# Down projections of two gated MLPs: where the folds of the weight blocks stand in VectorE's queue

## The chip, the cores and the metric

One core of one Trainium2 chip runs the whole kernel. The metric is the device time of one execution in microseconds; 2590.62 us is the median of three runs of the kernel before (2589.14 to 2591.91). An execution under the profiler took 2588.23 us, of which the profile shows a span of 2586.4 us from the first to the last instruction.

## The reference, cut to what matters

A trunk of two layers (a gated linear attention and a Fourier mixer), each followed by a gated MLP with a width-3 convolution, on 1024 latent and 128 context tokens of width 1024. The change lies in the last product of the MLP, which is computed once per layer:

```python
def conv_ffn(h, w_up, conv_w, conv_b, w_down, rows):
    a, g = jnp.split(h @ w_up, 2, axis=-1)
    ...
    return (jax.nn.silu(a) * g) @ w_down
```

`w_down` is 2816 x 1024 (2816 = 22 blocks of 128), and its product is added to the residual stream with a gate per channel.

## The kernel before

`ffn(l, ...)` computes the MLP of layer l. Its second half, the down projection, multiplies by a Strassen-Winograd scheme: the 1152 tokens are cut in two halves, the 22 row blocks of `w_down` in even and odd ones (11 pairs, `NP`), its 1024 columns in two halves. That gives four kinds of weight block (kind 0 to 3; `wd[kind, j]` is a 128 x 512 block of pair j), and seven products in place of eight. The loop over `steps` runs the first five products in the order `a2`, `s1`, `s4`, `a1`, `s2`, each over both slices of 288 tokens of its half, and then `s3` and `g2` once for each slice. Each step walks the 11 pairs, j = 0 to 10; a pair of a step is called a block here.

A block of a step needs three things before TensorE (PE) can run its 24 matmuls (4 column groups m, 2 slices s, 3 matmuls each on lines 97 to 99, since every fp32 operand is a high and a low part):

- a **stationary operand** (`stationary`): ScalarE (ACT) copies the weight block to its high part (L1073, `wd`), VectorE (DVE) subtracts to get the low part (L1074, `wd`, called "lo" here). Six buffers (tag "wh") hold them, so they run up to six blocks ahead of PE.
- a **moving operand** for each slice (`moving`): SyncE (SP) loads the slice (L1082, `hr`), ACT makes the high part (L1083, `hh`), DVE the low part (L1084, `hl`). Two pairs of buffers hold them, so `hh` and `hl` of block j + 2 have to wait until PE is through with block j.
- in `s1` and `s4`, and at the end of `s2`, a **fold** of the weight blocks in place (`fold`, L1064 on DVE): `s1` needs kind 2 plus kind 3 (one fold a pair); `s4` needs kind 1 minus (the sum less kind 0), two folds a pair, the second reading the first. A fold is one 128 x 512 instruction, or two of 128 x 256 for pair 10, whose halves lie in two pages: 12 fold instructions in `s1`, 24 in `s4`, in each layer.

At the end of each step, its sums are added into the residual pages: DVE reads PSUM or ACT's copy of it (L1165, `xd`; the copies are L1162, `room`). The next step's matmuls into the same PSUM bank wait for that.

The order of the work on an engine is set when the program is built: a scheduler takes instructions by priority as they become ready in its own model, and `tc.high_priority()` puts the operands of all blocks ahead of the matmuls. `tc.issue_after(ins)` keeps the instructions of its block behind `ins` in their engine's queue, and no more. Each engine then runs its queue strictly in that order. Before, all folds of a step are kept behind one instruction, `made[kind]`, the last lo of the step before (`behind`, fetched at j = 0):

```python
if j == 0 and what in ("s1", "s4"):
    behind = made[{"s1": 1, "s4": 2}[what]].ins
if what == "s1":
    with tc.issue_after(behind):
        fold(2, 3, ALU.add, j)
```

Weight blocks of kinds 1 to 3 are loaded in `a2`, those of kind 0, which `s4`'s first fold reads, during `s1` (`loads`, L1025 and L1034 on SP).

Of the kernel before, what the change touches and what calls it, by code (L numbers as in the profile page):

```python
# [15 lines left out]
F32 = mybir.dt.float32  # L16
# [4 lines left out]
ALU = mybir.AluOpType  # L21
# [24 lines left out]
def trunk(tc, a, o):  # L46
    nc = tc.nc
    V, S, G, PE = nc.vector, nc.scalar, nc.gpsimd, nc.tensor
# [16 lines left out]
    def mm_ps(name):  # L65
        return pp.tile([P, 512], F32, tag="mm", bufs=3, name=name)

    def at_ps(name):
        return pp.tile([P, 512], F32, tag="at", bufs=4, name=name)
# [156 lines left out]
    def feed(x, first, key, acc=None):  # L226

        n = key[1] - key[0]
        if first:
            accs[key] = sb.tile([P, CH], F32, tag="kt", bufs=3, name=f"acc{key[0]}") if acc is None else acc  # L230
            S.activation(accs[key][:, :n], x, AF.Square)
        else:
            sq = t15("sq")[:, :n] if n > SUB else sb.tile([P, SUB], F32, tag="sb", bufs=4, name="sq")[:, :n]
            S.activation(sq, x, AF.Square)
            V.tensor_tensor(accs[key][:, :n], accs[key][:, :n], sq, op=ALU.add)  # L235
# [743 lines left out]
    def ffn(l, xp, rs, xd, after, ahead=None, w=None, stages=None):  # L979
# [57 lines left out]
        def key(th, s):  # L1037
            return th * HT + s * SUB, th * HT + (s + 1) * SUB
# [22 lines left out]
        def fold(x, y, op, j, reverse=False):  # L1061

            for (c, xx), (_, yy) in zip(wd[x, j], wd[y, j]):
                V.tensor_tensor(xx, *((yy, xx) if reverse else (xx, yy)), op=op)  # L1064

        made = {}

        def stationary(kind, j, wt=None):
            if wt is None:
                wt = sb.tile([P, 1032], F32R, tag="wh", bufs=6, name=f"wd{l}")[:, :1024]  # L1070
            for c, x in wd[kind, j]:
                hi, lo = wt[:, c], wt[:, 512:][:, c]
                S.activation(hi, x, AF.Copy)  # L1073
                made[kind] = V.tensor_tensor(lo, x, hi.bitcast(F32), op=ALU.subtract)  # L1074
            return wt

        def moving(name, ss, j):
            hi, lo = (t30(n, F32R).rearrange("p a b -> p (a b)")[:, :HT] for n in ("hh", "hl"))
            for s in ss:
                c = slice(s * SUB, (s + 1) * SUB)  # L1080
                raw = t15("hr")[:, :SUB]
                nc.sync.dma_start(raw, hd[j][names.index(name), s])  # L1082
                S.activation(hi[:, c], raw, AF.Copy)  # L1083
                V.tensor_tensor(lo[:, c], raw, hi[:, c].bitcast(F32), op=ALU.subtract)  # L1084
            return hi, lo
# [12 lines left out]
        def room_for_kept():  # L1098
            pgs = [page(f"keep{i}", F32R) for i in range(7)]
            slots = [pg[:, 1024 * i:1024 * i + 1024] for pg in pgs for i in range(2)]  # L1100
            slots.insert(10, sb.tile([P, T], F32R, tag="w4", bufs=1, name="keep")[:, :1024])
            kept.update(zip([("s3", j) for j in range(NP)] + [("g2", j) for j in range(4)], slots))

        def products(m, what, ss, wt, hi, lo, first, last):
            for s in ss:
                c = slice(s * SUB, (s + 1) * SUB)
                mm3(pss[m, s][:, :SUB], (wt[:, m * P:(m + 1) * P], wt[:, 512 + m * P:512 + (m + 1) * P]),
                    (hi[:, c], lo[:, c]), first, last, skip=True)
        for n, (what, name, kind, (mh, th), ss) in enumerate(steps):
            if what in fresh:  # L1110
                for s in range(2):
                    for m in range(4):
                        pss[m, s] = at_ps("pd") if s else mm_ps("pd") if m < 3 else \
                            pp.tile([P, 512], F32, tag="md", bufs=1, name="pd")
            if ahead:
                ahead(n)
            elif n == 5:
                room_for_kept()
            held = []
            for j in range(NP):  # L1120
                for load, *args in loads.get((n, j), ()):
                    load(*args)
                with tc.high_priority():

                    if j == 0 and what in ("s1", "s4"):
                        behind = made[{"s1": 1, "s4": 2}[what]].ins

                    if what == "s1":
                        with tc.issue_after(behind):
                            fold(2, 3, ALU.add, j)  # L1130
                    elif what == "s4":
                        with tc.issue_after(behind):
                            fold(2, 0, ALU.subtract, j)
                            fold(1, 2, ALU.subtract, j)
                    wt = kept.get((what, j))
                    if wt is None or n < 7:
                        wt = stationary(kind, j, wt)
                    hi, lo = moving(name, ss, j)
                    if what == "s2":
                        fold(2, 3, ALU.subtract, j, reverse=True)  # L1140
                held.append((what, ss, wt, hi, lo, what in fresh and j == 0, j == NP - 1))

                if n < len(steps) - 1 or j != NP - 2:
                    for m in range(4):
                        for args in held:
                            products(m, *args)
                    held = []
                if n == 7 and j == 5:
                    norms = after(X, xp, rs, key(1, 0), key(0, 0))
                if n == 8 and j == 5:  # L1150
                    norms = after(X, xp, rs, key(1, 1))
                if n > 6 and j > 4 and j != 6 or n == 8 and j < 5:
                    next(norms, None)
            room = sb.tile([P, T], F32, tag="w4", bufs=1, name="room") if len(ss) > 1 else None
            for m in range(4):
                x = Xw(4 * mh + m)
                for s in ss:
                    t0, t1 = key(th, s)
                    got = pss[m, s][:, :SUB]
                    if s and room is not None:  # L1160
                        copied = room[:, m * SUB:(m + 1) * SUB]
                        S.activation(copied, got, AF.Copy)  # L1162
                        got = copied
                    for c0, c1, c in [(t0, t1, 0)] if t1 <= LAT else [(t0, LAT, 0), (LAT, t1, 1)]:
                        V.scalar_tensor_tensor(x[:, c0:c1], got[:, c0 - t0:c1 - t0], gate(4 * mh + m, c),  # L1165
                                               x[:, c0:c1], op0=ALU.mult, op1=ALU.add)
            if final_of[mh, th] == what:
                for s in ss:
                    k = key(th, s)
                    for m in range(4 * mh, 4 * mh + 4):  # L1170
                        feed(Xw(m)[:, slice(*k)], k not in accs, k, acc1[s] if th else None)
# [8 lines left out]
    def after0(X, xp, rs, *keys):  # L1180
        for key in keys:
            save_x(xp, xs_dram, slice(*key))
        yield from rstd_steps(rs, *keys)
    xp, X, Xw, rs = ffn(0, xp, rs, xs, after0, fold_operands, early["w"], early["ops"])


# [77 lines left out]
    for pr_ in range(2):  # L1264
# [5 lines left out]
        for typ in range(2):  # L1270
# [15 lines left out]
            for i in range(6):  # L1286
                off = (i % 2) * 1024 + typ * 512
                hi, lo = (dat[i // 2][:, off + h:off + h + 256].rearrange("p (g n) -> p g n", g=2) for h in (0, 256))
# [11 lines left out]
        def pqv(pq, g, typ, hl, half):  # L1300
            i = (g * 2 + typ) * 4 + hl * 2 + half
            return pq[i // 6][:, (i % 6) * CH:(i % 6 + 1) * CH]
# [4 lines left out]
        for half in range(2):  # L1307
            tw = weight(a["dft_t"][half], 1024, f"dt{half}{pr_}")
            for typ in range(2):
# [5 lines left out]
                for g, ny in todo:  # L1315
# [12 lines left out]
                    else:  # L1328
                        hi, lo = pqv(pq, g, typ, 0, half), pqv(pq, g, typ, 1, half)
# [14 lines left out]
    for m in range(KT):  # L1344
        with tc.high_priority():
            raw = raw_w(a["fwo"][m], 1024, f"fo{m}")
            whl = [sb.tile([P, 1032], F32R, tag="wh", bufs=6, name=f"fw{i}") for i in range(2)]
            for typ in range(2):
# [5 lines left out]
                hi, lo = (w[:, typ * 512:typ * 512 + 512] for w in whl)  # L1354
# [17 lines left out]
        x = Xw(m)  # L1372
# [48 lines left out]
    for _ in norm:  # L1421
        pass
    ffn(1, xp, rs, xs, final)
    ctx.close()

# [133 lines left out]
```

## Time and profile before

| | before |
|---|---|
| median of 3 runs | 2590.62 us |
| the profiled execution | 2588.23 us |
| its span | 2586.4 us |
| PE busy | 2429.6 us, 94% |
| DVE busy | 1844.4 us, 71% |
| ACT busy | 1090.3 us, 42% |
| mean granted TensorE clock | 0.977 |
| the DVE folds, L1064 | 96 instructions, 88 + 8 |

Reading it: PE is the engine that is nearly always busy, so time is what keeps PE idle or slows its clock. A matmul of 288 columns follows the one before it after some 0.13 us at the full clock (granted 1.00, which is 2.4 GHz) and 0.24 us at the lower level (0.50, 1.2 GHz). The down projection of layer 0 runs from about 1260 to 1490 us, that of layer 1 from about 2297 us to the end. In the rows further down, a number in brackets is the idle time of the engine just before the instruction, with what ended it.

### The profile page before, as it was taken

What the parts mean: (1) busy time and instruction counts of PE and PEld (TensorE: products, weight loads), DVE (VectorE), ACT (ScalarE), POOL (GpSimd) and SP (SyncE); (2) the same over time, 40 slices, a digit from 0 to 9 for tenths busy, and PEclk for the clock granted to TensorE, in tenths of its full rate; (3) what the DMA queues carried; (4) which work ended last, traced back from release to release, by engine and by line L of the source; (5) the groups of instructions that cost most, each with busy time, mean ns of one, the idle gap of its engine ahead of it and who ended that gap; (6) DMA issues with size and microseconds to landing.
All of it is one profiled execution on the core that took longest, in us unless ns stands there. A gap on an engine that the chain in (4) does not pass through costs nothing. (4 is left out here: it accounts for less than half of the span.)

```text
span 2586.4 us, 46546 instructions
## 1 busy us (share of the span) xinstructions
PE 2429.6 (94%) x18122; PEld 2332.2 (90%) x18122; DVE 1844.4 (71%) x3339; ACT 1090.3 (42%) x2086; POOL 732.9 (28%) x548
## 2 busy tenths in 40 slices
PE   6999999988999999999989998999899999998997
PEld 5998988887999899999989996998899999998997
DVE  7647384666698677777766877287987777787676
ACT  5435343444364233333335564344533333333453
POOL 3435344543103334344100005330144444410000
PEclk9999999998999999999999998999999999999999
DMA  7213222104334443323754347343223232375334
GB/s 261 74 48 93 81 88 79 54 21 145 109 108 126 155 137 99 114 82 101 242 178 134 113 153 214 102 166 134 94 79 115 82 114 82 98 240 176 93 84 126
DMA packets 200972, 309.85 MB, mean 120 GB/s; under 512 B 18288, under 2 KB 142064, under 8 KB 200752
## 3 DMA queue, kind: packets, MB, share of 16 engines
q1 hardware_dynamic: 196528, 302.66, 36.8%
q10 hardware_dynamic: 4224, 4.23, 0.5%
q8 instruction: 142, 2.33, 0.4%
q14 instruction: 78, 0.64, 0.1%
HBM read 233.71 MB, written 73.11 MB: 119 GB/s over the span
## 5 line engine op out<-in xcount | busy, mean ns | idle before, releaser
L98 PE MATMUL pd<-hl,wd 128*128 128x288 f32 x1112 | 331.9, 301 | 28.7 <-DVE hl L1084 28.5
L99 PE MATMUL pd<-hh,wd 128*128 128x288 f32 x1112 | 329.9, 300 | 0.0
L97 PE MATMUL pd<-hh,wd 128*128 128x288 f32 x1112 | 317.6, 299 | 5.5 <-ACT hh L1083 3.2
L98 PEld LDWEIGHTS pd<-hl,wd 128*128 128x128 f32 x1112 | 213.7, 192 | 31.2 <-DVE hl L1084 30.7
L809 POOL TENSOR_TENSOR s<-wa,s 128x512 fp32r<-128x512 f32 x114 | 157.3, 1380 | 278.4 <-ACT s L808 278.4
L1084 DVE TENSOR_TENSOR hl<-hr,hh 128x288 fp32r<-128x288 f32 x308 | 138.3, 454 | 133.8 <-ACT hh L1083 133.5
L1083 ACT ACTIVATE hh<-hr 128x288 fp32r<-128x288 f32 x308 | 133.4, 437 | 233.7 <-PE pd L98 218.8
L97 PEld LDWEIGHTS pd<-hh,wd 128*128 128x128 f32 x1112 | 205.6, 189 | 10.1 <-ACT hh L1083 5.3
L99 PEld LDWEIGHTS pd<-hh,wd 128*128 128x128 f32 x1112 | 213.1, 192 | 0.0
L809 POOL TENSOR_TENSOR a<-wa,a 128x512 fp32r<-128x512 f32 x76 | 100.0, 1316 | 332.4 <-ACT a L808 231.0
L808 ACT ACTIVATE s<-wa 128x512 fp32r<-128x512 f32 x120 | 75.5, 630 | 190.7 <-DVE wa L826 114.7
L977 ACT ACTIVATE hid<-hid 128x576 f32<-128x576 f32 x88 | 60.4, 686 | 157.1 <-DVE hid L972 100.5
L1074 DVE TENSOR_TENSOR wd<-wd,wd 128x512 fp32r<-128x512 f32 (+1 forms) x184 | 116.4, 642 | 9.9 <-ACT wd L1073 4.9
L1073 ACT ACTIVATE wd<-wd 128x512 fp32r<-128x512 f32 (+1 forms) x184 | 104.6, 580 | 26.7 <-DVE wd L1064 14.9
L808 ACT ACTIVATE a<-wa 128x512 fp32r<-128x512 f32 x80 | 50.4, 631 | 142.8 <-PE pa L99 75.9
L1209 POOL TENSOR_TENSOR fn<-fn 128x512 f32<-128x512 f32 x8 | 14.1, 1762 | 330.9 <-ACT wp L728 311.1
L860 DVE TENSOR_TENSOR q<-q,ps 128x288 f32<-128x288 f32 x232 | 98.5, 445 | 11.3 <-PE ps L99 9.7
L535 POOL TENSOR_TENSOR le<-vbr 128x384 f32<-128x384 f32 x72 | 74.3, 1036 | 109.3 <-PE lv L549 93.7
L97 PE MATMUL pa<-fh1x,a 128*128 128x288 f32 x320 | 95.4, 298 | 5.7 <-DVE c L860 3.3
L541 POOL TENSOR_TENSOR le<-le,qk 128x384 f32<-128x384 f32 x72 | 89.4, 1246 | 36.6 <-ACT le L540 35.1
L860 DVE TENSOR_TENSOR c<-q,pa 128x288 f32<-128x288 f32 x80 | 36.1, 451 | 87.7 <-PE pa L99 87.7
L97 PE MATMUL ps<-fh1x,s 128*128 128x288 f32 x320 | 95.2, 298 | 3.0 <-DVE hid L917 3.0
(689 smaller groups left out, 8917.3 us busy)
## 6 DMA issues: line engine op xcount, KB each, us to landing
hr<-hid SPq DMA_DIRECT2D x308, 144.0 KB, 2.2
wm<-in_wmod SPq DMA_DIRECT2D x112, 256.0 KB, 2.8
hid<-hid SPq DMA_DIRECT2D x44, 576.0 KB, 3.9
wa<-in_wup SPq DMA_DIRECT2D x40, 512.0 KB, 3.5
wg<-in_wup SPq DMA_DIRECT2D x40, 512.0 KB, 4.1
hid<-t SPq DMA_DIRECT2D x132, 144.0 KB, 3.3
wd<-in_wdn SPq DMA_DIRECT2D x16, 1024.0 KB, 8.4
wm<-in_wmod SPq DMA_DIRECT2D x96, 128.0 KB, 3.4
```

Source lines behind the costliest of these rows:

```text
L97: PE.matmul(ps, lhsT=wh, rhs=xh, start=first, stop=False, skip_group_check=skip)
L98: PE.matmul(ps, lhsT=wh, rhs=xl, start=False, stop=False, skip_group_check=skip)
L99: PE.matmul(ps, lhsT=wl, rhs=xh, start=False, stop=last, skip_group_check=skip)
L535: G.tensor_tensor(view(e, 0, [2 * s, nb], [s, 2], [1, s]), ref, view(bb, 0, [2 * s, nb], [CH + s, 2], [1, s]), op=ALU.subtract)
L541: G.tensor_tensor(e[:, 0], e[:, 0], qk[:, base:base + CH], op=ALU.mult)
L808: S.activation(w[name][:, :512], x, AF.Copy)
L809: (eng or G).tensor_tensor(w[name][:, 512:], x, w[name][:, :512].bitcast(F32), op=ALU.subtract)
L860: add.last = V.tensor_tensor(out[:, xs], x[:, xs], ps[s][:, :SUB], op=op)
L1073: S.activation(hi, x, AF.Copy)
L1074: made[kind] = V.tensor_tensor(lo, x, hi.bitcast(F32), op=ALU.subtract)
L1083: S.activation(hi[:, c], raw, AF.Copy)
L1084: V.tensor_tensor(lo[:, c], raw, hi[:, c].bitcast(F32), op=ALU.subtract)
```

## The change

`made` becomes a list to which `stationary` appends its last lo. In `s1` and `s4` the folds of pair j are kept behind `made[-3]`, the lo three stationary operands before the one that needs them, in place of all behind one. No instruction is added, removed or resized.

```diff
-        made = {}
+        made = []
...
-                made[kind] = V.tensor_tensor(lo, x, hi.bitcast(F32), op=ALU.subtract)
+                low = V.tensor_tensor(lo, x, hi.bitcast(F32), op=ALU.subtract)
+            made.append(low.ins)
             return wt
...
-                    if j == 0 and what in ("s1", "s4"):
-                        behind = made[{"s1": 1, "s4": 2}[what]].ins
 
                     if what == "s1":
-                        with tc.issue_after(behind):
+                        with tc.issue_after(made[-3]):
                             fold(2, 3, ALU.add, j)
                     elif what == "s4":
-                        with tc.issue_after(behind):
+                        with tc.issue_after(made[-3]):
                             fold(2, 0, ALU.subtract, j)
                             fold(1, 2, ALU.subtract, j)
```

What that does to the queues stands at three places, all in layer 0; layer 1 has the same pattern. In the names, wd_0 and wd_1 are pages of kind 1, wd_3 and wd_4 of kind 0, wd_5 and wd_6 of kind 2, wd_8 and wd_9 of kind 3, wd_2 and wd_7 hold pairs 8 and 9 of several kinds; a wd with five digits is a stationary operand. Line numbers of the changed kernel are one higher from 1075 to 1126 and one lower behind that (hl is L1085, xd is L1164).

**Place 1**, DVE's queue where `a2` ends and `s1` begins. Before, behind the lo of `a2`'s last block (wd_13102):

```order
L1074 TENSOR_TENSOR wd_13102<-wd_1_12689,wd_13102 128x256
L1064 TENSOR_TENSOR wd_5_12693<-wd_5_12693,wd_8_12696 128x512 x2
L1064 TENSOR_TENSOR wd_6_12694<-wd_6_12694,wd_9_12697 128x512 x3
L1064 TENSOR_TENSOR wd_5_12693<-wd_5_12693,wd_8_12696 128x512
L1064 TENSOR_TENSOR wd_6_12694<-wd_6_12694,wd_9_12697 128x512
L1064 TENSOR_TENSOR wd_5_12693<-wd_5_12693,wd_8_12696 128x512
L1074 TENSOR_TENSOR wd_13163<-wd_5_12693,wd_13163 128x512
L1064 TENSOR_TENSOR wd_7_12695<-wd_7_12695 128x512 x2
L1084 TENSOR_TENSOR hl<-hr,hh 128x288
L1064 TENSOR_TENSOR wd_5_12693<-wd_5_12693,wd_8_12696 128x256
L1064 TENSOR_TENSOR wd_6_12694<-wd_6_12694,wd_9_12697 128x256
L1084 TENSOR_TENSOR hl<-hr,hh 128x288 x3
```

And now, from the same lo on:

```order
L1074 TENSOR_TENSOR wd_13102<-wd_1_12689,wd_13102 128x256
L1064 TENSOR_TENSOR wd_5_12693<-wd_5_12693,wd_8_12696 128x512
L1085 TENSOR_TENSOR hl<-hr,hh 128x288 x2
L1074 TENSOR_TENSOR wd_13163<-wd_5_12693,wd_13163 128x512
L1064 TENSOR_TENSOR wd_5_12693<-wd_5_12693,wd_8_12696 128x512
L1085 TENSOR_TENSOR hl<-hr,hh 128x288 x2
L1074 TENSOR_TENSOR wd_13201<-wd_5_12693,wd_13201 128x512
L1064 TENSOR_TENSOR wd_6_12694<-wd_6_12694,wd_9_12697 128x512
```

Twelve folds stood between that lo and the low parts of `a2`'s blocks 6 to 8; now one fold stands behind each lo, and the first two have gone further ahead, into `a2`'s own lo's.

**Place 2**, DVE's queue where `s1` gives way to `s4`: before, the end of the 24 folds and what follows them.

```order
L1064 TENSOR_TENSOR wd_2_12690<-wd_2_12690,wd_7_12695 128x512
L1064 TENSOR_TENSOR wd_1_12689<-wd_1_12689,wd_6_12694 128x512
L1064 TENSOR_TENSOR wd_0_12688<-wd_0_12688,wd_5_12693 128x256
L1064 TENSOR_TENSOR wd_1_12689<-wd_1_12689,wd_6_12694 128x256
L1074 TENSOR_TENSOR wd_13611<-wd_0_12688,wd_13611 128x512
L1084 TENSOR_TENSOR hl<-hr,hh 128x288 x4
L1074 TENSOR_TENSOR wd_13650<-wd_0_12688,wd_13650 128x512
L1084 TENSOR_TENSOR hl<-hr,hh 128x288 x2
```

And now, from the lo of `s1`'s block 8 (wd_13476) on:

```order
L1074 TENSOR_TENSOR wd_13476<-wd_7_12695,wd_13476 128x512
L1064 TENSOR_TENSOR wd_5_12693<-wd_5_12693,wd_3_12691 128x512
L1085 TENSOR_TENSOR hl<-hr,hh 128x288
L1064 TENSOR_TENSOR wd_0_12688<-wd_0_12688,wd_5_12693 128x512
L1085 TENSOR_TENSOR hl<-hr,hh 128x288
L1074 TENSOR_TENSOR wd_13514<-wd_7_12695,wd_13514 128x512
L1064 TENSOR_TENSOR wd_5_12693<-wd_5_12693,wd_3_12691 128x512
L1085 TENSOR_TENSOR hl<-hr,hh 128x288
```

Each lo is followed by the two folds of one pair, with a low part of the moving operand behind each of them.

**Place 3**, the tail of `s4`'s folds in the changed kernel, with buffer numbers. DVE's queue from the low part of `s4`'s block 2, slice 0 (hl_13697) on; wd0_13849 and wd0_13888 are the stationary operands of blocks 6 and 7, hl_13736 is block 3:

```order
L1085 TENSOR_TENSOR hl_13697<-hr_13698,hh_13696 128x288
L1074 TENSOR_TENSOR wd0_13849<-wd0_1_12689,wd0_13849 128x512
L1064 TENSOR_TENSOR wd0_7_12695<-wd0_7_12695,wd0_2_12690 128x512
L1074 TENSOR_TENSOR wd0_13888<-wd0_1_12689,wd0_13888 128x512
L1064 TENSOR_TENSOR wd0_5_12693<-wd0_5_12693,wd0_3_12691 128x256
L1064 TENSOR_TENSOR wd0_6_12694<-wd0_6_12694,wd0_4_12692 128x256
L1064 TENSOR_TENSOR wd0_2_12690<-wd0_2_12690,wd0_7_12695 128x512
L1064 TENSOR_TENSOR wd0_0_12688<-wd0_0_12688,wd0_5_12693 128x256
L1064 TENSOR_TENSOR wd0_1_12689<-wd0_1_12689,wd0_6_12694 128x256
L1085 TENSOR_TENSOR hl_13736<-hr_13737,hh_13735 128x288
L1085 TENSOR_TENSOR hl_13697<-hr_13702,hh_13696 128x288
```

And PE's queue there, from the last two of the eight matmuls on lines 98 and 99 that block 2's slice 0 has:

```order
L98 MATMUL pd_13157<-hl_13697,wd0_13693 128x288
L99 MATMUL pd_13157<-hh_13696,wd0_13693 128x288
L97 MATMUL pd_13154<-hh_13735,wd0_13732 128x288
L97 MATMUL pd_13158<-hh_13696,wd0_13693 128x288
L97 MATMUL pd_13159<-hh_13696,wd0_13693 128x288
L97 MATMUL pd_13160<-hh_13696,wd0_13693 128x288
L97 MATMUL pd_13161<-hh_13696,wd0_13693 128x288
L97 MATMUL pd_13155<-hh_13735,wd0_13732 128x288
L97 MATMUL pd_13156<-hh_13735,wd0_13732 128x288
L97 MATMUL pd_13157<-hh_13735,wd0_13732 128x288
L98 MATMUL pd_13154<-hl_13736,wd0_13732 128x288
```

Here the last folds have not been spread: five of them stand in one row behind the lo of block 7, ahead of three low parts of blocks 2 and 3, and PE has eight matmuls on high parts alone ahead of the first that reads hl_13736. Before, no fold stood between these low parts.

## Rows read from the trace of the kernel before

**Rows 1.** The page: the span, and PE's busy time, share and instructions.

```profile
span 2586.4 us, 46546 instructions
...
PE 2429.6 (94%) x18122; PEld 2332.2 (90%) x18122; DVE 1844.4 (71%) x3339; ACT 1090.3 (42%) x2086; POOL 732.9 (28%) x548
```

**Rows 2.** Waits of PE, 1230 to 1450 us: total us, times, longest us.

```profile
PE pd L98 <- DVE hl L1084: 14.3, 3, 10.1
```

**Rows 3.** Timeline of PE: start, us, instruction, idle before it and its releaser.

```profile
1262.05 0.40 PE L97 MATMUL pd<-hh,wd 128*128 128x288 f32 x1 [0.69 <-DVE c L860]
1263.02 0.40 PE L98 MATMUL pd<-hl,wd 128*128 128x288 f32 x1 [0.57 <-DVE hl L1084]
...
1289.22 0.61 PE L98 MATMUL pd<-hl,wd 128*128 128x288 f32 x1 [3.68 <-DVE hl L1084]
...
1337.11 0.98 PE L98 MATMUL pd<-hl,wd 128*128 128x288 f32 x2 [10.08 <-DVE hl L1084]
...
2323.63 0.40 PE L98 MATMUL pd<-hl,wd 128*128 128x288 f32 x1 [3.48 <-DVE hl L1084]
...
2369.18 0.97 PE L98 MATMUL pd<-hl,wd 128*128 128x288 f32 x2 [10.09 <-DVE hl L1084]
```

**Rows 4.** Windows: length, then busy us and count of PE, PEld, DVE, ACT, POOL; granted clock, DMA share, GB/s.

```profile
1262.00:1266.50 4.50, 3.88 (x18) 3.67 (x19) 3.77 (x8) 1.22 (x4) 0.00 (x0) 0.69 0.93 288
...
1289.20:1294.50 5.30, 5.28 (x22) 5.29 (x23) 2.06 (x6) 1.23 (x3) 0.00 (x0) 0.50 0.72 215
...
1300.00:1327.00 27.00, 27.00 (x203) 26.73 (x201) 18.55 (x39) 11.61 (x28) 0.00 (x0) 1.00 0.93 298
...
1337.10:1342.20 5.10, 5.09 (x20) 5.02 (x21) 2.21 (x5) 1.30 (x3) 0.00 (x0) 0.50 0.39 114
...
2324.00:2328.00 4.00, 4.00 (x33) 4.00 (x32) 1.83 (x4) 1.72 (x5) 0.00 (x0) 1.00 0.87 270
...
2369.20:2374.00 4.80, 4.80 (x22) 4.72 (x23) 2.18 (x5) 1.30 (x3) 0.00 (x0) 0.60 0.38 103
```

**Rows 5.** Timeline of DVE: the folds where `s1` and `s4` are prepared.

```profile
1281.19 4.89 DVE L1064 TENSOR_TENSOR wd<-wd,wd 128x512 f32<-128x512 f32 x8
...
1289.08 0.75 DVE L1064 TENSOR_TENSOR wd<-wd,wd 128x256 f32<-128x256 f32 x2
...
1322.62 13.47 DVE L1064 TENSOR_TENSOR wd<-wd,wd 128x512 f32<-128x512 f32 x24
...
2354.69 13.46 DVE L1064 TENSOR_TENSOR wd<-wd,wd 128x512 f32<-128x512 f32 x24
```

**Rows 6.** Timeline of DVE: one block of `s1` without a fold.

```profile
1347.00 0.46 DVE L1084 TENSOR_TENSOR hl<-hr,hh 128x288 fp32r<-128x288 f32 x1 [1.54 <-ACT hh L1083]
1347.52 0.69 DVE L1074 TENSOR_TENSOR wd<-wd,wd 128x512 fp32r<-128x512 f32 x1
1348.13 0.45 DVE L1084 TENSOR_TENSOR hl<-hr,hh 128x288 fp32r<-128x288 f32 x1
```

**Rows 7.** Timeline of DVE: `s2` in layer 0, one fold in each block.

```profile
1412.70 0.69 DVE L1064 TENSOR_TENSOR wd<-wd,wd 128x512 f32<-128x512 f32 x1
1414.38 0.46 DVE L1084 TENSOR_TENSOR hl<-hr,hh 128x288 fp32r<-128x288 f32 x1 [0.99 <-ACT hh L1083]
```

**Rows 8.** Timeline of DVE: `s2` in layer 1, lo's of two consecutive blocks.

```profile
2443.36 0.69 DVE L1074 TENSOR_TENSOR wd<-wd,wd 128x512 fp32r<-128x512 f32 x1
...
2446.70 0.69 DVE L1074 TENSOR_TENSOR wd<-wd,wd 128x512 fp32r<-128x512 f32 x1
```

**Rows 9.** Timeline of DVE: first sums of `s1` read out, and block 2 of `s4`.

```profile
1350.57 0.51 DVE L1165 SCALAR_TENSOR_TENSOR xd<-pd,modT,xd 128x288 f32<-128x288 f32 x1
...
1357.58 0.46 DVE L1084 TENSOR_TENSOR hl<-hr,hh 128x288 fp32r<-128x288 f32 x1 [0.61 <-ACT hh L1083]
```

**Rows 10.** Timeline of SP, the first load of kind 0 in layer 0.

```profile
1301.14 1.02 SPq L1025 DMA_DIRECT2D wd<-in_wdn  x1
```

**Rows 11.** The tile wd, 1255 to 1345 us: its loads from issue to landing.

```profile
DMA to landing us min/median/max: 4.0/5.4/8.4
```

## The prediction

> **What bounds the kernel now.** I read the page first: PE is busy for 2429.6 of 2586.4 us [rows 1], so there are at most some 157 us in which anything but PE sets the time, and the question is how many of them the folds cause. The waits of PE in layer 0's down projection come next: the whole stretch has 14.3 us of waiting for DVE's `hl`, in three waits [rows 2]. The timeline of PE shows where they are: 0.57 us at the start of `a2`, 3.68 us before 1289.22 and 10.08 us before 1337.11 [rows 3]. These three add up to 14.33, so there is no other wait of that kind. Layer 1 repeats the two long ones, 3.48 and 10.09 us.
>
> The timeline of DVE tells what `hl` was late for. Eight folds begin at 1281.19, 24 at 1322.62, 24 at 2354.69 [rows 5]: the long waits are the times in which DVE worked through its folds with the next low parts queued behind them. With two pairs of moving buffers PE has about two blocks in hand, 2 x 24 matmuls; the 13.47 us of 24 folds use that up and leave 10 us of nothing.
>
> The windows show a second cost: after three of the four long waits PE comes back at the lower clock. The 5.30 us behind the first have a granted clock of 0.50 and 22 matmuls, the 5.10 us behind the second 0.50 and 20, the 4.80 us behind the last 0.60 and 22; only the 3.48 us wait is followed by 1.00 [rows 4].
>
> **The change, part by part.** No instruction comes or goes, so all that counts is where DVE's queue moves, and what SP and ACT do with it.
>
> *The waits that go.* 3.68 + 10.08 + 3.48 + 10.09 = 27.3 us [rows 3]. Clock: 64 matmuls took 5.30 + 5.10 + 4.80 = 15.2 us; at the 27.00 us for 203 matmuls of an undisturbed stretch, 0.133 each, they take 8.5 us [rows 4]. That is 6.7 us. Together 34.0 us; this is the most that the change can give, since PE computes the same matmuls without a break on either side.
>
> *The folds in their new places.* A fold of 512 columns costs 0.61 us of DVE (4.89 us for 8), one of 256 about 0.34 [rows 5]. In a block of 24 x 0.133 = 3.2 us DVE does one lo (0.61, from 1347.52 to 1348.13) and two `hl` of at most 0.46, and then idles 1.54 us until ACT, and behind it PE, lets it go on [rows 6]. In `s1` one fold (0.61) goes into that idle time and in `s4` two (1.22). The kernel already has the first case: the blocks of `s2` hold one fold each and still show 0.99 us of idle time [rows 7]. By the same rows two folds leave 0.3 to 0.4 us. So I cost them at nothing; the cover is that idle time. If it goes, the price is bounded by layer 1's `s2`, where a fold and two lo's share a block and the lo's of consecutive blocks are 3.34 us apart in place of 3.2 [rows 8]: 0.15 us x 11 blocks x 2 layers = 3.3 us. I take 0, because [rows 7] is the same step with the same operands, and keep 3.3 for the range. A gain from the moved folds beyond the waits is excluded: PE has none left there.
>
> *The end of `s4`'s folds (place 3).* Here the spreading fails. Behind the low part of block 2's slice 0, DVE now has lo, fold, lo, five folds and only then block 3's low part: 3 x 0.61 + (0.61 + 4 x 0.34) + 0.46 = 4.3 us, less 0.1 since an instruction starts that much before the one ahead of it ends (0.69 long, 0.61 apart [rows 6]): 4.2 us. From the same point PE's queue has eight matmuls of block 2 and eight on high parts alone, 16 x 0.133 = 2.1 us. The difference, 2.1 us, is a new wait in each layer. That the chain starts on time follows from [rows 9]: before, with the readouts of `s1` in the same queue, block 2's low part still idled 0.61 us for ACT's `hh`; now two folds of 0.61 more stand ahead of it, but its own `hh` also comes later, since PE finishes block 0 only after the last readout. Bounds of this wait: 0, if PE is late itself, and 3.2 us, if the eight matmuls on high parts can't start. I take 2.1, the difference of the two queues as they are written: 4.2 us for both layers.
>
> *The clock after the new wait.* A fall costs 6.7 / 3 = 2.2 us. Waits of 0.69 and 0.57 us in quick succession went with a mean clock of 0.69 in the 4.50 us around them, and 3.68 us cost the clock, yet 3.48 us did not [rows 3, 4]. So 2.1 us can go either way; I count one fall for the two layers, 2.2 us, with 0 and 4.4 as bounds. The Trainium skill, "TensorE: Matmul & The Clock Gate", section "HAM oscillation", warns of gaps between bursts of matmuls, because the PE then starts the next burst at the lower clock and pays for the warming again each time. [...] The trace agrees with it for three of four long waits, and its 3.48 us wait disagrees.
>
> *The first folds (place 1)* stand in `a2`, where DVE also finishes the last pair of the up projection; one fold of 0.61 a block fits as above, and three that don't would cost 1.8 us a layer. I take 0 and leave the 1.8 to the range. *SP:* the loads of kind 0 that `s4`'s first fold reads are issued during `s1`, from 1301.14, and land 4.0 to 8.4 us later [rows 10, 11], at 1309.5 at the latest. That fold now stands behind the lo of `s1`'s block 8, two blocks before the old burst: 1322.62 - 6.4 = 1316.2, less the 5.9 us (3.68 + 2.2) that `s1` starts earlier, is 1310.3. So it is in time even if SP issues it no earlier; SP's queue goes with DVE's, so it should.
>
> *Sum.* 34.0 - 4.2 - 2.2 = 27.6 us off the profiled execution's 2588.23, which is 2560.6; the median of the runs shown stands 2.4 us above that execution, so **2563.0 us**. What is late next is the five folds of place 3.
>
> **The rivals.**
>
> *DVE becomes the bound of `s1` and `s4`.* Two folds leave DVE 0.3 to 0.4 us a block, and at the turn to `s4` eleven readouts come on top. In favour: layer 1's `s2` runs at 3.34 us a block [rows 8]. Against: it has a lo more. Price: the 3.3 us above, and a wait of 3.2 instead of 2.1 us in place 3 with a fall of the clock each time (2 x 1.1 + 2.2): 2563.0 + 7.7 = 2570.7, up to some 2574 if the readouts are late too and PE waits for PSUM.
>
> *The clock falls behind both new waits.* In favour: it fell behind three of the four long waits [rows 4], and behind a pair that add up to 1.26 us [rows 3]. Against: it did not behind 3.48 us. The time is 2563.0 + 2.2 = 2565.2 us, and 2560.8 if it falls behind neither; I give the first 0.27, the second 0.17, and both lie in the forecast's own band. [...]
>
> *The change gives little, because the gain is swallowed.* If the start of `s1` were set by the transfers and not by DVE, layer 0's part would go. In favour: the DMA share is 0.93 from 1300 to 1327, at 298 GB/s [rows 4]. Against: PE was busy for all 27.00 us of that stretch, and every long wait ended with DVE [rows 3]. If the waits before `s1` come back with their clock (3.68 + 3.48 + 2.2 = 9.4 us) and half of those before `s4` (10.1 us), 34.0 - 9.4 - 10.1 - 4.2 = 10 us are left: 2580, and in the worst case no change.
>
> *Slower: `s4`'s first fold waits for its load.* In the new queue it stands ahead of low parts of `s1`'s blocks 4 and 5; if kind 0 hasn't landed, DVE stops and PE runs dry after about 1.5 us. Each microsecond of lateness costs one per layer. It decides from 1310.3 us on, and eats all of a layer's gain (14 us) when the load lands about 15 us later than that, 24 us after its issue. In favour: the margin is only 0.8 us by the slowest landing; DMA is at 0.93. Against: the longest landing of that tile is 8.4 us [rows 11]. At 20 us late per layer the time would be about 2600.
>
> **How the numbers follow.** Forecast, with its clock cases, 2558 to 2567: 0.72. DVE as the bound, 2567 to 2574: 0.16. Gain swallowed, 2574 and more: 0.09, of which 0.04 within 0.2% of the time before (5.2 us, about what a measurement of this kernel can tell from no change). Slower: 0.03. The range goes from 2557 (34.0 us and nothing given back) to 2571, the rival's own value, and leaves out some 2 in 10. Faster by over 0.2%: 0.72 + 0.16 + 0.05 = 0.93; the same 0.04; slower 0.03.
>
> **What would show it.** In the changed kernel's profile: no waits of 3 us or more for `hl` at 1289, 1337, 2323 and 2369 us, folds in ones and twos on DVE's timeline, one new wait of about 2 us for `hl` in each layer early in `s4`, behind five folds, with the granted clock at 0.50 behind it in one layer of the two, and otherwise no idle time of PE in `s1` and `s4`. Wrong would be: blocks of `s4` further apart than 3.2 us, a fold that waits for DMA, or a PE that waits for a readout (`xd`, L1164).

## The result

The changed kernel takes 2561.16 us (median of 4 runs, 2557.18 to 2564.86) where the kernel before took 2591.26 beside it: a ratio of 0.9882 with a 95% interval of 0.986 to 0.9903. Its profiled execution took 2564.86 us, 23.4 less than that of before.

The page: the span, the engines, and the group of matmuls that [rows 2] is about, which idled 28.7 us in all before.

```profile
span 2563.0 us, 46543 instructions
...
PE 2425.1 (95%) x18122; PEld 2329.2 (91%) x18122; DVE 1841.2 (72%) x3339; ACT 1089.3 (43%) x2086; POOL 730.9 (29%) x548
...
L98 PE MATMUL pd<-hl,wd 128*128 128x288 f32 x1112 | 328.7, 299 | 5.4 <-DVE hl L1085 5.2
```

The timeline of PE has this in place of the four long waits of [rows 3]; the first two lines are the first matmul on the low part ahead of the wait, and the last eight matmuls that PE had left. Besides these, layer 1 has one wait for `hl` of 0.36 us, before 2329.88, where `a2` gives way to `s1`.

```profile
1345.21 0.33 PE L98 MATMUL pd<-hl,wd 128*128 128x288 f32 x1
...
1346.31 1.22 PE L97 MATMUL pd<-hh,wd 128*128 128x288 f32 x8
1349.34 0.40 PE L98 MATMUL pd<-hl,wd 128*128 128x288 f32 x1 [1.82 <-DVE hl L1085]
...
2369.01 0.48 PE L98 MATMUL pd<-hl,wd 128*128 128x288 f32 x1 [1.85 <-DVE hl L1085]
```

DVE while PE is in `s1`, in a block into which two of `s4`'s folds have moved (the first two lines), and then DVE just before 1349.34:

```profile
1328.52 0.46 DVE L1085 TENSOR_TENSOR hl<-hr,hh 128x288 fp32r<-128x288 f32 x1 [0.39 <-ACT hh L1084]
...
1331.70 0.46 DVE L1085 TENSOR_TENSOR hl<-hr,hh 128x288 fp32r<-128x288 f32 x1 [0.39 <-ACT hh L1084]
...
1344.61 0.46 DVE L1085 TENSOR_TENSOR hl<-hr,hh 128x288 fp32r<-128x288 f32 x1 [0.61 <-ACT hh L1084]
...
1346.89 2.03 DVE L1064 TENSOR_TENSOR wd<-wd,wd 128x256 f32<-128x256 f32 x5
1348.83 1.19 DVE L1085 TENSOR_TENSOR hl<-hr,hh 128x288 fp32r<-128x288 f32 x3
```

These blocks are 3.18 us apart, and DVE still idles 0.39 us in each. The one place where folds pile up is the five behind 1346.89: 4.22 us from one low part to the next, and PE waits 1.82 of them.

The windows of the changed kernel around the start of `a2`, behind the wait in layer 0 and behind that in layer 1 (the third column from the end is the granted clock):

```profile
1265.40:1270.00 4.60, 3.96 (x16) 3.75 (x17) 3.79 (x9) 1.20 (x3) 0.00 (x0) 0.64 0.92 288
1349.30:1353.00 3.70, 3.66 (x27) 3.66 (x28) 2.22 (x5) 1.30 (x3) 0.00 (x0) 1.00 0.51 130
2369.00:2374.00 5.00, 4.99 (x26) 5.00 (x27) 2.21 (x5) 1.30 (x3) 0.00 (x0) 0.66 0.37 105
```

The clock falls behind one of the two new waits, and at the start of `a2`, as it did before.

To add it up, the windows from `a2`'s first wait to the wait of 1.17 to 1.18 us for `hh` in `s3`, in both layers, of the kernel before and then of the changed one. Length less PE's busy time is idle time. The number of matmuls is the same, so PE's busy time rises where they run at the lower clock, and by short delays: a matmul shows as 0.29 us long and the next one starts 0.13 us behind it, so one that starts up to 0.16 us late leaves no idle time.

```profile
1262.05:1463.84 201.79, 186.20 (x1337) 184.30 (x1338) 142.39 (x298) 91.15 (x214) 0.00 (x0) 0.95 0.53 160
2299.19:2463.45 164.26, 149.20 (x1096) 147.57 (x1097) 114.35 (x241) 71.17 (x170) 0.00 (x0) 0.97 0.51 156
```

```profile
1265.46:1451.18 185.72, 182.05 (x1337) 179.82 (x1338) 142.04 (x298) 90.95 (x214) 0.00 (x0) 0.99 0.57 174
2287.26:2440.45 153.19, 149.49 (x1097) 147.47 (x1097) 114.26 (x241) 70.96 (x170) 0.00 (x0) 0.99 0.54 167
```

The two stretches went from 366.05 to 338.91 us, 27.1 less: 23.3 of it idle time (30.7 to 7.4), 3.9 PE's busy time (335.4 to 331.5), which is what the clock gave back less new short delays. Such a delay, at the turn from `s1` to `s4`, with 0.29 us from start to start and no idle time noted:

```profile
1344.28 0.29 PE L99 MATMUL pd<-hh,wd 128*128 128x288 f32 x1
1344.57 0.40 PE L97 MATMUL pd<-hh,wd 128*128 128x288 f32 x1
```

The rest of the profiled execution got 3.7 us longer; 3.4 of that lies ahead of `a2`, where the queues are the same, so it is what differs between executions. In the fourteen profiles of this document `a2` starts between 1262.05 and 1269.27 us; the kernel before is the earliest.

### The profile page after: what moved, and what is told of

It reads as the page before. It is cut to its first block, busy times and chain, and to the rows that moved or that the text cites. A ratio compares the mean times of both kernels' runs of the same rounds, so it can differ in the third digit from the quotient of the medians.

```text
span 2563.0 us, 46543 instructions
## 1 busy us (share of the span) xinstructions
PE 2425.1 (95%) x18122; PEld 2329.2 (91%) x18122; DVE 1841.2 (72%) x3339; ACT 1089.3 (43%) x2086; POOL 730.9 (29%) x548
## 5 line engine op out<-in xcount | busy, mean ns | idle before, releaser
L1085 DVE TENSOR_TENSOR hl<-hr,hh 128x288 fp32r<-128x288 f32 x308 | 138.5, 455 | 109.3 <-ACT hh L1084 108.7
L97 PE MATMUL ps<-fh0t,s 128*128 128x288 f32 x320 | 96.4, 302 | 1.4 <-DVE c L860 1.4
```

The costliest lines, as they stand in the source:

```text
L97: PE.matmul(ps, lhsT=wh, rhs=xh, start=first, stop=False, skip_group_check=skip)
```

## The experiments

Each was timed beside the kernel before. "Stretches", "idle" and "PE busy" are the sums just shown, in us, of the profiled execution.

| kernel | median | ratio to before, interval | stretches | idle | PE busy |
|---|---|---|---|---|---|
| before | | | 366.1 | 30.7 | 335.4 |
| changed | 2561.2 | 0.9882 (0.9860 to 0.9903) | 338.9 | 7.4 | 331.5 |
| e9, changed again | 2560.8 | 0.9867 (0.9850 to 0.9884) | 337.4 | 7.3 | 330.1 |
| e1, `s1` undone | 2575.9 | 0.9931 (0.9910 to 0.9952) | 353.3 | 15.6 | 337.8 |
| e2, `s4` undone | 2583.2 | 0.9952 (0.9934 to 0.9970) | 355.6 | 23.7 | 331.8 |
| e3, four ahead | 2559.9 | 0.9870 (0.9849 to 0.9892) | 333.4 | 4.8 | 328.6 |
| e11, the same | 2560.8 | 0.9869 (0.9851 to 0.9887) | 333.9 | 5.0 | 328.8 |
| e4, tail late | 2558.7 | 0.9860 (0.9838 to 0.9881) | 333.3 | 3.8 | 329.6 |
| e10, the same | 2556.5 | 0.9852 (0.9832 to 0.9872) | 331.6 | 3.7 | 328.0 |
| e5, six ahead | 2574.6 | 0.9933 (0.9919 to 0.9947) | 351.9 | 16.7 | 335.2 |
| e6, eight ahead | 2579.2 | 0.9948 (0.9932 to 0.9964) | 348.8 | 15.3 | 333.5 |
| e7, one more | 2564.8 | 0.9891 (0.9872 to 0.9909) | 343.1 | 9.8 | 333.2 |
| e8, two more | 2575.6 | 0.9940 (0.9928 to 0.9953) | 349.6 | 16.6 | 332.9 |
| e12, threes | 2561.5 | 0.9881 (0.9862 to 0.9901) | 338.3 | 9.5 | 328.8 |

(In e5 and e6 the stretch of layer 1 begins 0.6 and 1.8 us later in the work, behind a longer first wait.)

**One half undone at a time.** In e1 the folds of `s1`, in e2 those of `s4` stand behind one lo, as before; in both, `behind` is fetched at j = 0.

```diff
+                    if j == 0:
+                        behind = made[-1] if made else None
...
-                        with tc.issue_after(made[-3]):
+                        with tc.issue_after(behind):
```

> The folds of s1 all behind the last lo of a2, as before; those of s4 stay spread. Theory (each burst of folds starves PE by itself): the waits of 3.68 and 3.48 us for hl come back where s1 begins, one of them with a fall of the clock (2.2 us), 7.2 + 2.2 = 9.4 us (7.2 to 11.6); the waits of 10 us stay away and those of 1.8 us early in s4 stay. So some 18 us faster than the kernel before, 9 us slower than the changed one. Rival (the start of s1 is set by the transfers): the waits come back with another releaser or not at all, and the time is the changed kernel's within 2 us.

> The folds of s4 all behind the last lo of s1, as before; those of s1 stay spread. Theory: two waits of 10.1 us for hl where s4 begins, each with a fall of the clock, and no wait of 1.8 us behind it: 20.2 + 4.4 - 3.7 - 2.2 = 18.7 us slower than the changed kernel, 9 us (7 to 12) faster than the kernel before. Rival (half of the waits before s4 is lost anyway): some 9 us slower than the changed kernel.

Timeline of PE, e1:

```profile
1292.00 0.61 PE L98 MATMUL pd<-hl,wd 128*128 128x288 f32 x1 [4.19 <-DVE hl L1085]
1354.41 0.48 PE L98 MATMUL pd<-hl,wd 128*128 128x288 f32 x1 [1.84 <-DVE hl L1085]
...
2317.92 0.61 PE L98 MATMUL pd<-hl,wd 128*128 128x288 f32 x1 [4.32 <-DVE hl L1085]
2380.99 0.40 PE L98 MATMUL pd<-hl,wd 128*128 128x288 f32 x1 [1.84 <-DVE hl L1085]
```

And e2:

```profile
1332.92 0.98 PE L98 MATMUL pd<-hl,wd 128*128 128x288 f32 x2 [10.08 <-DVE hl L1085]
...
2363.51 0.98 PE L98 MATMUL pd<-hl,wd 128*128 128x288 f32 x2 [10.10 <-DVE hl L1085]
```

Each half brings back its own waits and only those, with DVE as the releaser. The stretches of e2 are 16.7 us longer than the changed kernel's (18.7 expected, with falls of 2.2 us). Those of e1 are 14.4 longer, more than expected (9.4, at most 11.6): its waits are 0.5 and 0.8 us longer than in [rows 3], and the clock fell behind all four. Neither half of the gain is swallowed: the start of `s1` is not set by the transfers. They have a small share in these waits: one of the folds in the burst stands until the load of its weights lands, for 0.81 us in layer 0 of the kernel before and for 0.49 and 0.82 us in e1. That of e1, layer 1:

```profile
2315.53 1.29 DVE L1064 TENSOR_TENSOR wd<-wd 128x512 f32<-128x512 f32 x2 [0.82 <-DMA wd<-in_wdn]
```

In the changed kernel DVE waits for no load in either stretch.

**The tail of `s4`'s folds.** e3 and e11 queue all folds four ahead, e4 and e10 those of `s4`'s last two pairs one ahead.

```diff
-                        with tc.issue_after(made[-3]):
+                        with tc.issue_after(made[-4]):
```

```diff
-                        with tc.issue_after(made[-3]):
+                        with tc.issue_after(made[-1 if j > 8 else -3]):
                             fold(2, 0, ALU.subtract, j)
```

> The changed kernel with the folds four stationary operands ahead in place of three. In DVE's queue the tail between the low part of s4's block 2, slice 0, and that of block 3 is then lo, three folds of 256 columns, lo, one of 256: 0.61 x 2 + 4 x 0.34 + 0.46 = 3.0 us in place of lo, fold, lo, five folds, 4.2 us. Theory (the wait of 1.8 us is this queue less what PE has in hand, 2.4 us): 0.6 us of wait in each layer, 2.4 us less, and 2.2 us more if the clock holds: 2.4 to 4.6 us faster than the changed kernel. Rival (PE is late itself there, or any lead does): the same within 1 us. Rival (kind 0 comes too late for a fold one block earlier): DVE waits for a DMA before the first fold of s4, and a wait of 1 to 3 us appears in s1: slower by up to 6 us.

> The changed kernel with the folds of s4's pairs 9 and 10 one stationary operand ahead, all others three. The queue between the low parts of s4's blocks 2 and 3 is then two lo's and no fold, 2 x 0.61 + 0.46 = 1.7 us, less than the 2.4 us that PE has in hand. Theory: both waits of 1.8 us go, and with them the one fall of the clock: 3.7 + 2.2 = 5.9 us faster than the changed kernel (3.7 without the clock), some 33 us faster than the kernel before. Rival (the wait belongs to the turn of PSUM from s1 to s4, not to the folds): the wait stays with another releaser and the time is the changed kernel's within 1 us. Rival (the late folds of pairs 9 and 10 hold up the last low parts of s4): new waits for hl near the end of s4, 2 us a layer slower.

> The changed kernel once more, beside the next two on one chip. Its ratio to the kernel before should be that of its first measurement, 0.988; waits for hl of 1.8 us early in s4 in both layers. Whether the granted clock falls behind them is open: in four kernels with this same wait (the changed one, with one more and with the folds of s1 undone) it fell behind five of six.

> The folds of s4's pairs 9 and 10 one stationary operand ahead, again. Theory: 3.7 to 5.9 us faster than the changed kernel on the same chip, a ratio to it of 0.998; no wait for hl early in s4. If the time beside the changed kernel is the same, the waits that go are given back outside the rows read so far.

> All folds four stationary operands ahead, again: two waits of 0.65 us early in s4, without a fall of the clock: 2.4 us of wait and 1.7 to 3.4 us of clock less than the changed kernel, a ratio to it of 0.998.

The same stretch of DVE's timeline in e3, and then in e10:

```profile
1345.61 0.46 DVE L1085 TENSOR_TENSOR hl<-hr,hh 128x288 fp32r<-128x288 f32 x1 [0.54 <-ACT hh L1084]
1346.13 0.69 DVE L1074 TENSOR_TENSOR wd<-wd,wd 128x512 fp32r<-128x512 f32 x1
1346.74 1.09 DVE L1064 TENSOR_TENSOR wd<-wd,wd 128x256 f32<-128x256 f32 x3
...
1348.69 1.19 DVE L1085 TENSOR_TENSOR hl<-hr,hh 128x288 fp32r<-128x288 f32 x3
```

```profile
1345.44 0.46 DVE L1085 TENSOR_TENSOR hl<-hr,hh 128x288 fp32r<-128x288 f32 x1 [0.61 <-ACT hh L1084]
1345.90 1.29 DVE L1074 TENSOR_TENSOR wd<-wd,wd 128x512 fp32r<-128x512 f32 x2
1347.11 1.19 DVE L1085 TENSOR_TENSOR hl<-hr,hh 128x288 fp32r<-128x288 f32 x3
```

From one low part to the next it is 4.22 us in the changed kernel, 3.08 in e3 and 1.67 in e10. PE's waits there, in e3:

```profile
1349.19 0.40 PE L98 MATMUL pd<-hl,wd 128*128 128x288 f32 x1 [0.65 <-DVE hl L1085]
...
2361.61 0.40 PE L98 MATMUL pd<-hl,wd 128*128 128x288 f32 x1 [0.64 <-DVE hl L1085]
```

In e4 and e10 there is none. So 4.22 goes with a wait of 1.82, 3.08 with 0.65, 1.67 with none: the wait is DVE's queue less 2.4 us, and the folds in it are its cause, not the turn of PSUM. The clock stays up in both stretches of e3, e10 and e11 (in e4 it falls once, at the start of `a2`), and the stretches of e10 are 5.8 us shorter than those of e9, of e4 5.6 and of e3 5.5 shorter than those of the changed kernel.

In the whole time this is not resolved (a ratio to the changed kernel of 0.998 was expected): beside e9's 2560.8 us, e10 has 2556.5 and e11 2560.8, and the intervals overlap. e4 and e10 are the version with the lowest median and the fewest waits; that it beats the changed kernel is shown in the stretches only. That it beats the kernel before is shown: 0.9852.

**More lead: the load of kind 0.** e5 and e6 put -6 and -8 in place of -3, at both places.

> The changed kernel with the folds six stationary operands ahead. The first fold of s4 now stands right behind the readouts of a2, the last of which began at 1306.36 us in the changed kernel, so at about 1306.9; the loads of kind 0 that it reads were issued there at 1302.38 and take 3.5 us at the least, 4.5 at the median, 8.4 for the slow ones: they land at 1305.9, 1306.9 or 1310.8. Theory of the rival that was on the other side (a fold that comes before its load stops DVE, and PE behind it): DVE idles for a DMA in front of that fold, 0 to 4 us, and PE waits for hl what exceeds the 2.4 us or more that it has in hand, 0 to 1.5 us a layer. Early in s4 the readouts now come behind the last folds, so no wait of 1.8 us. In all between 6 us faster than the changed kernel (no wait at all) and as fast. If loads don't matter: no idle time of DVE for a DMA, 4 to 6 us faster.

> The changed kernel with the folds eight stationary operands ahead, two more than there are buffers for them. DVE then has ten folds of s4 and two lo's in a row behind a2's readouts, ahead of the low parts of s1: 12 x 0.61 + 0.46 = 7.8 us, and the first of them may wait for kind 0 as well. Theory (bunch less cover): 7.8 less the 2.4 to 4.5 us that PE has in hand: 3.3 to 5.4 us of wait in each layer, with the clock some 11 to 15 us slower than the changed kernel less the 3.7 to 5.9 us of early s4, where the last bunch is one of four; 5 to 11 us slower. If the load of kind 0 is late too, as many us more per layer as DVE idles for it. Rival (more lead is never worse): as fast as with four, or faster than the changed kernel.

SP and DVE of e5: kind 0's first load, and `s4`'s first fold.

```profile
1301.13 0.38 SPq L1025 DMA_DIRECT2D wd<-in_wdn  x1
...
1309.13 0.69 DVE L1064 TENSOR_TENSOR wd<-wd,wd 128x512 f32<-128x512 f32 x1 [2.81 <-DMA wd<-in_wdn]
```

And PE of e5, layer 0:

```profile
1266.44 0.61 PE L98 MATMUL pd<-hl,wd 128*128 128x288 f32 x1 [1.87 <-DVE hl L1085]
1310.25 0.40 PE L98 MATMUL pd<-hl,wd 128*128 128x288 f32 x1 [1.38 <-DVE hl L1085]
1315.57 0.40 PE L98 MATMUL pd<-hl,wd 128*128 128x288 f32 x1 [1.41 <-DVE hl L1085]
1322.70 0.40 PE L98 MATMUL pd<-hl,wd 128*128 128x288 f32 x1 [0.51 <-DVE hl L1085]
...
1344.20 0.40 PE L98 MATMUL pd<-hl,wd 128*128 128x288 f32 x1 [2.24 <-DVE hl L1085]
```

The fold stops DVE for 2.81 us (3.33 in layer 1) until the load lands 8.0 us after its issue, and PE behind it, as the rival on the slower side had it. The expected total is missed by far: 13 us slower than the changed kernel, not as fast or faster. What I left out: the folds of two pairs now come together (waits of 0.40 to 0.54 at every second block), the last ones stand right ahead of the readouts (2.24 us), and the first fold of `s1` waits 0.61 us for a load ahead of `a2`'s low parts (1.87 us). In e6 ten folds stand in a row, with two lo's between them, and the first six begin behind a load:

```profile
1310.96 3.70 DVE L1064 TENSOR_TENSOR wd<-wd,wd 128x512 f32<-128x512 f32 x6 [2.01 <-DMA wd<-in_wdn]
```

```profile
1318.69 0.61 PE L98 MATMUL pd<-hl,wd 128*128 128x288 f32 x1 [5.60 <-DVE hl L1085]
...
2334.14 0.40 PE L97 MATMUL pd<-hh,wd 128*128 128x288 f32 x1 [2.87 <-DVE xd L1164]
```

Its stretches are 10 us longer, 12 with the later beginning of layer 1's, but the profiled execution, 2571.5 us, was the fastest of its five. By the medians e6 is 18 us slower than the changed kernel, and the 5 to 11 that were expected are too few. What the theory left out are longer waits at the start of `a2` (3.84 and 2.38 us, in place of 0.57 and 0.58), and in layer 1 a readout that PE waits for. Beyond four, more lead is not better.

**More work for DVE.** e7 has one more instruction of a fold's size behind each of eight pairs of `s4`, e8 two.

```diff
                             fold(1, 2, ALU.subtract, j)
+                            for _ in range(1 if j < 8 else 0):
+                                V.tensor_tensor(wd[1, j][0][1], wd[1, j][0][1], wd[1, j][0][1], op=ALU.max)
```

> The changed kernel with one more DVE instruction of a fold's size (128 x 512 of kind 1, the maximum of the block with itself, in place, which leaves it as it is) behind the folds of s4's pairs 0 to 7, in each layer. Theory (two folds leave DVE 0.39 to 0.41 us of idle time in a block of 3.18): a third, 0.61, exceeds it by 0.2 us a block, 1.7 us in eight blocks, which the two blocks that PE has in hand still cover, but for the turn to s4: 0 to 2 us a layer, 0 to 4 us slower than the changed kernel. Rival (DVE already bounds these blocks): 8 x 0.61 us a layer, 10 us slower.

> The same with two more such instructions a pair. Theory: 1.22 less 0.40 us is 0.8 us a block, 6.6 us in eight blocks, of which PE has 2.4 us or more in hand: 2 to 4 us of wait in each layer with one or two falls of the clock each, 8 to 16 us slower than the changed kernel, as waits for hl at the end of s1 and the turn to s4. Rival (DVE already bounds): 20 us slower. Rival (DVE has more room than its idle time shows): no change.

The same 20 us of the changed kernel, of e7 and of e8 (PE is the first busy time, DVE the third):

```profile
1320.00:1340.00 20.00, 20.00 (x151) 19.81 (x150) 17.68 (x35) 9.22 (x22) 0.00 (x0) 1.00 0.62 193
```

```profile
1320.00:1340.00 20.00, 19.91 (x148) 19.44 (x146) 19.83 (x38) 9.22 (x22) 0.00 (x0) 1.00 0.56 179
```

```profile
1320.00:1340.00 20.00, 16.24 (x119) 15.54 (x117) 19.70 (x38) 6.50 (x15) 0.00 (x0) 1.00 0.48 160
```

With two folds a block DVE is busy for 17.7 of 20 us; with three it is full and PE still runs; with four PE loses 3.8 of 20 us. The stretches grow by 4.2 and 10.6 us (0 to 4 and 8 to 16 expected). So inside a block the moved folds cost nothing because of idle time that was there, and that room is smaller than one more fold.

**Bunches of three pairs.** e12 fetches `made[-3]` only at every third pair of `s4`; pairs 9 and 10 become one bunch of their own by this, so its expectation is wrong about them.

```diff
+                        if j in (0, 3, 6, 9):
+                            behind = made[-3]
...
-                        with tc.issue_after(made[-3]):
+                        with tc.issue_after(behind):
```

> The changed kernel with the folds of s4 in bunches of three pairs (pairs 0 to 2 behind one lo, 3 to 5 behind another, 6 to 8 behind a third; pairs 9 and 10 as in the changed kernel). A bunch of six is 3.7 us, with the lo's around it and the first hl 0.61 + 3.7 + 0.61 + 0.46 = 5.4 us. Theory (wait = bunch less what PE has in hand, which was 14.5 less 10.1, 4.4 us, for the burst of 24, and 7.2 less 4.2, 3.0 us, for that of s1 undone): three waits of 1 to 2.4 us a layer beside the one of 1.8, 6 to 14 us, and a fall of the clock behind some of them (1.7 us each): 8 to 20 us slower than the changed kernel. Rival (only the sum of the folds in a step counts, or a bunch of six is covered): the changed kernel's time within 1 us.

PE of e12, layer 0; layer 1 has the same four waits within 0.01 us:

```profile
1316.81 0.40 PE L98 MATMUL pd<-hl,wd 128*128 128x288 f32 x1 [0.42 <-DVE hl L1085]
1327.08 0.40 PE L98 MATMUL pd<-hl,wd 128*128 128x288 f32 x1 [0.45 <-DVE hl L1085]
1338.08 0.40 PE L98 MATMUL pd<-hl,wd 128*128 128x288 f32 x1 [1.69 <-DVE hl L1085]
1348.99 0.40 PE L98 MATMUL pd<-hl,wd 128*128 128x288 f32 x1 [0.45 <-DVE hl L1085]
```

The theory's numbers fall: not 8 to 20 us slower, but the changed kernel's time. The first two bunches, of 5.4 us, cost 0.4 each, so in the middle of `s1` PE has some 5 us in hand, not 3 to 4.4. The third is as long and costs 1.69, at the end of `s1`: there PE goes on when the third of the low parts behind the bunch is done (1338.02), in the others when the first is.

```profile
1336.83 1.19 DVE L1085 TENSOR_TENSOR hl<-hr,hh 128x288 fp32r<-128x288 f32 x3
```

The last wait has the changed kernel's place and 4.28 us of DVE's queue, and is 0.45 long: PE's timeline has 28 matmuls from that low part to the wait, where the changed kernel has 16. What PE has in hand is a matter of the place, and must be counted there.

## Why the prediction was right

The time, 2561.2 us, lies 1.8 below the forecast of 2563.0 and inside its own band; the likeliest case came, and in the main for its reasons. That it came so close is partly luck: the four runs spread over 7.7 us, and two terms of the sum were off in opposite directions.

- *The waits that go, 27.3 us.* All four are gone; e1 and e2 bring back each pair by itself. One reading beside them was wrong, though nothing in the sum rests on it: PE didn't have two blocks in hand. Two blocks are 6.4 us, and 13.47 us of folds that leave 10.08 of waiting cover 3.4.
- *The clock, 2.2 us a fall.* Right for the falls that went, too much for the new one. A fall is a stretch behind a wait in which the granted clock is 0.50. From PE's return until its matmuls are 0.13 us apart again, the three falls of [rows 4], before:

```profile
1289.22:1294.57 5.35, 5.35 (x22) 5.35 (x23) 2.11 (x6) 1.30 (x3) 0.00 (x0) 0.51 0.71 212
1337.11:1342.35 5.24, 5.24 (x21) 5.16 (x22) 2.20 (x5) 1.30 (x3) 0.00 (x0) 0.51 0.39 113
2369.18:2373.19 4.01, 4.01 (x16) 3.93 (x17) 1.66 (x4) 1.30 (x3) 0.00 (x0) 0.52 0.38 110
```

  and the new one of the changed kernel:

```profile
2369.01:2372.62 3.61, 3.61 (x15) 3.61 (x16) 1.14 (x3) 0.93 (x3) 0.00 (x0) 0.53 0.42 123
```

  At 0.133 us a matmul the excess is 2.4, 2.4 and 1.9 us, 6.8 together (6.7 forecast), and 1.6 for the new fall, which is shorter. The fall at the start of `a2` costs 1.6 in both kernels.
- *The folds in their new places, 0.* Right inside the blocks, with the cover named: 0.39 us of idle time a block, 0.3 to 0.4 forecast, blocks 3.18 us apart. The margin is as thin as it was said to be (e7, e8). Not quite right at the turn from `s1` to `s4`: matmuls start 0.03 to 0.17 us late there, 0.7 to 0.8 us in each layer. The changed kernel, e1 and e10 have these delays; before and e2, with the burst of 24, have none there. Whether the spread folds make them, or the long wait of the burst had hidden them, isn't shown.
- *The new wait in place 3, 4.2 less 2.1.* It came in both layers, behind the five folds, 1.82 and 1.85 long. DVE's queue was 4.22; PE's was 2.4, not 2.1. In the trace a matmul is 0.29 us long and the next starts 0.13 after it, so the last of 16 ends 0.16 later than the count says, and the first begins 0.14 after its low part (1344.61 + 0.46 to 1345.21). That the wait is this difference is shown by e3 and e10; PE has the same 16 matmuls there in e3.
- *One fall behind two waits.* So it was, in layer 1; but it was a count taken between none and two, not a rule: the same wait in e9, e1 and e7 gave one fall, two and two.
- *First folds and the load of kind 0.* The load cost nothing, the first folds at most the 0.36 us of layer 1. The margin of the load was 0.8 us by the forecast. In the changed kernel it is issued at 1302.38 and lands 6.8 us later, and `s4`'s first fold starts at 1313.73, a margin of 4.5 us (5.4 in layer 1).
- *The sum.* 27.6 forecast, 27.1 in the two stretches: 23.3 of idle time against 27.3 - 4.2 = 23.1, some 5.1 of clock against 6.7 - 2.2 = 4.5, and some 1.3 given back in short delays, against nothing. The profiled executions differ by less, 23.4, and the medians beside each other by more, 30.1; the stretches are the part that the change can touch.

Of the rivals, DVE as the bound is refuted by e7, where a third fold fills DVE and costs 4.2 us in the stretches, not the 10 that a bound engine would take; the turn to `s4`, where it expected trouble, gave the short delays, at a fifth of its price. The swallowed gain is refuted by e1 and e2. The load that comes too late is a real mechanism, shown by e5, three operands further ahead than the change goes.

## What to carry to other kernels

Work that is queued in one block on an engine with idle time stops whoever waits for the next short result on that engine; spread over the idle times it costs next to nothing as long as each piece fits into one. The price of a bunch is its length in that queue less what the waiting engine has in its own queue at that place, and both can be counted from the order of the two queues. How far ahead to put the pieces has two ends: too late and they bunch at the end, too early and they wait for their own loads in front of work that was ready.

## What the runs showed that was not expected

- The length of a wait alone doesn't tell whether the clock falls. Behind the waits of 1.80 to 1.85 us early in `s4` the granted clock fell to 0.50 in six of eight cases (changed, e1, e7 and e9, two layers each), behind the 1.69 us of e12 in none of two, behind the 0.63 to 0.65 us of e3 and e11 in none of four. Elsewhere it fell behind 2.24 and 2.25 us in e5, but not behind 2.38 in e6 or 3.48 in the kernel before. At the start of `a2`, the waits of 0.68 to 0.69 and 0.56 to 0.57 us were followed by a fall in four of twelve executions of the same code. The Trainium skill, "TensorE: Matmul & The Clock Gate", section "HAM oscillation", tells of a kernel in which each wait of some 3 to 5 us between bursts of matmuls brought the lower clock. Here the waits of 3.54 us and more agree and the one of 3.48 us doesn't, and the clock also fell behind shorter waits than that page's. What decides is left open.
- The waits of e1 were 0.5 and 0.8 us longer than those of before with the same order of DVE's queue, and DVE's waits for transfers account for it. In layer 1 it stood 0.82 us inside the burst, where before it stood for nothing. In layer 0 it stood 1.37 us for a transfer of the up projection (`t`) ahead of the burst and 0.49 inside it, before 0.54 and 0.81, which is 0.5 more. Neither was varied by itself.
